# A PEER transformer layer on one core: low halves of early expert tiles made by a product, two PSUM banks for gates, one lookup traced later

## The chip, the core and the metric

The kernel runs on one core of a Trainium2 chip. The core has five engines with one instruction queue each: TensorE (PE, matrix products, with weight loads shown as PEld), VectorE (DVE), ScalarE (ACT), GpSimd (POOL) and SyncE (SP), and 16 DMA engines that all queues share. Each engine works off its queue in order; work on different engines is ordered by semaphores. The metric is the device time of one execution in microseconds (us), lower is better; of several runs the median counts.

## The reference

One layer of a diffusion backbone over 1024 latent tokens and 256 context tokens of width 1024. After the token mixers and their projection, `x1 = x + ...`, comes a PEER feed-forward part, the part that matters here:

```
h2 = modulate(rmsnorm(x1))                       # 1024 x 1024
q  = h2 @ wq                                     # 8 heads, two halves of 128
s1, s2 = q halves against 128 keys each;  top 16 of each half
cand = 16 x 16 sums per head;  top 16 of them    # 8 heads x 16 = 128 experts per token
gate = softmax(top 16);  expert = 128*i1 + i2    # of 16384 experts
act  = gelu(h2 . u[expert])                      # u, v: 16384 x 1024 each
out  = sum over the 128 chosen of gate * act * v[expert]
```

The result is `rmsnorm(x1 + mod * out)`.

## The kernel before

Operands of the large products are split into two fp16 halves, high and low (`hi = fp16(s*x)`, `lo = fp16(s*x - hi)`), and `mm3` (L97) makes three fp16 products of them. The tokens are eight blocks of 128. After the mixers and the merge, a first choice (`choosing(0)`, then `route`, the lookup of expert numbers for one block) runs beside the merge and output projection of the second half of the tokens.

Then the feed-forward part is done in two ways at once:

* For blocks 2, 3, 5, 6, 7 (`DB`) densely. `u` is 128 tiles of 128 experts. For each tile `u_load` fetches it, `u_turn` transposes it on TensorE into two PSUM tiles `put` (four 128x128 transposes each) and makes `uT`, high and low halves; `u_act` multiplies it with `h2` (24 products of 256 columns into `ph0`, 24 of 384 into `ph1`) and takes gelu. The dense gates come from one-hot matrices: for four tokens at a time VectorE makes `oh` (two instructions), TensorE multiplies eight 128x128 products into one PSUM tile `pgm`, ScalarE copies it to `gs`. A block has 32 such groups.
* For blocks 0, 1, 4 (`GB`) by gathering. Each of 768 steps is an indirect DMA that GpSimd issues (a "gather": 128 rows of u or v, one per token, into one of `AHEAD` = 6 buffers `row`), and one VectorE instruction that uses it: a dot product with `h2n` for rows of u (L979), an accumulation into `gacc` for rows of v (L984).

An early stage (about 1900 to 2820 us in the profile) runs the gates of blocks 2 and 3, the second choice (`choosing(1)`, eight heads of top-16 searches on VectorE) and the gates of blocks 5, 6, 7. Between these a planner in the code slips in early u tiles: each step of the stage yields a price in us (1.65 for a group of gates, 3.3 and 1.5 in the choice, 14 for a lookup), and for each `U_US` = 6.5 us one `early_tile()` is traced, followed by `G_E` gathers on average. 75 tiles are made so and stored in `act_d`. A late stage (2890 to 4100 us) runs over 32 groups of four v tiles, splits them, weighs the activations (reloaded as `acr`) with the gates, multiplies (`pe`), adds on VectorE into `acc`, makes the remaining u tiles, and spreads the gathers that are left evenly.

The order of instructions on each engine is set by a scheduler that takes what is ready first. Two marks bind it: a gather's issue on GpSimd is queued behind `pace` (the last low-half subtraction of `u_turn`, also on GpSimd), and its use on VectorE behind `vmark`, the last gate or accumulation instruction.

`uf` (L1026) is a float32 copy of the scaled `put` in SBUF, from which GpSimd subtracts `hi` (L1027). `first_half` is the generator of the first choice and the lookups of blocks 0, 1 and 2; `CS` says how many of its steps are taken per merge step, per output-projection tile and in the norm.

Of the kernel before, what the change touches and what calls it, by code (L numbers as in the profile page):

```python
# [1 line left out]

# [16 lines left out]
P = 128  # L19
# [19 lines left out]
SU = 64.0  # L39
# [5 lines left out]
TB = 4  # L45
# [22 lines left out]
def tile_layer(ctx: ExitStack, tc: tile.TileContext, x, c, ctxt, c_ctx, ada_w, ada_b, norm_mix_g,  # L68
# [3 lines left out]
    V, S, G, PE = nc.vector, nc.scalar, nc.gpsimd, nc.tensor  # L72
# [30 lines left out]
    const = pool(ctx, "const")  # L103
    dram = pool(ctx, "dram", space=DRAM)
    ident = const.tile([P, P], F32, name="ident")
    make_identity(nc, ident)
    ones = const.tile([P, P], F32, name="ones")
    V.memset(ones, 1.0)
    eps = const.tile([P, 1], F32, name="eps")
    V.memset(eps, EPS)  # L110
# [62 lines left out]
    with ExitStack() as mixers:  # L173
# [704 lines left out]
        def out_proj(hf, yT, fill=None):  # L878
            tiles = []
            for i in range(4):  # L880
                n = hf * 4 + i
                xt = mg.tile([P, D], F32, name=f"xr{n}", tag="xr", bufs=4)
                ld(out=xt, in_=x[n * P:(n + 1) * P, :])
                for h2 in range(2):
                    cs = slice(h2 * 512, (h2 + 1) * 512)
                    ps = pp.tile([P, 512], F32, name=f"pso{n}_{h2}", tag="pj", bufs=2)
                    mm3(ps, lambda k: yT[:, k, 0, i * P:(i + 1) * P], lambda k: yT[:, k, 1, i * P:(i + 1) * P],
                        lambda k: wo[:, 0, k, cs], lambda k: wo[:, 1, k, cs])
                    tm = mg.tile([P, 512], F32, name=f"tm{n}_{h2}", tag="tm")
                    tt(V, tm, ps, mod2[:, cs], ALU.mult)  # L890
                    tt(G, xt[:, cs], xt[:, cs], tm, ALU.add)
                st_(out=x1_d[n * P:(n + 1) * P, :], in_=xt)
                tiles.append(xt)
                if fill is not None:
                    for _ in range(CS[1]):
                        next(fill, None)
            return tiles

        def h2_rows(hf):
# [12 lines left out]

            return rows_of

        def next_norm(hf, tiles, fill=None):
            ss = rms_cols(tiles, mg, f"x1_{hf}")
            if fill is not None:
                for _ in range(CS[2]):
                    next(fill, None)
            norm_T(tiles, ss, lambda s, k: hb[hf][:, s, k, :], lambda k: cols2[:, 1, k:k + 1], lambda k: cols2[:, 0, k:k + 1],  # L920
                   mg, pp, f"m{hf}_", h2_rows(hf))

        yin = load_y(0)
        yT = mg.tile([P, KC, 2, HT], F16, name="yT0", tag="yT")
# [6 lines left out]
        yT = mg.tile([P, KC, 2, HT], F16, name="yT1", tag="yT")  # L931
# [8 lines left out]

        first_half = first()
        for j in range(KC):
            for _ in range(CS[0]):
                next(first_half, None)
            merge_step(1, j, yin, yT)
        next_norm(1, out_proj(1, yT, first_half), first_half)
        for _ in first_half:
            pass
        if "x1" in dbg:
# [22 lines left out]
    def gathering():  # L972

        held = []

        def use(n, s, row, h2n, dots):
            with tc.issue_after(vmark[0].ins):
                if h2n is not None:
                    V.scalar_tensor_tensor(out=row, in0=row, scalar=1.0, in1=h2n, op0=ALU.mult, op1=ALU.mult,  # L979
                                           accum_out=dots[:, s:s + 1])  # L980
                elif s == 0:
                    tsc(V, gacc[n], row, dots[:, s:s + 1], ALU.mult)
                else:
                    V.scalar_tensor_tensor(out=gacc[n], in0=row, scalar=dots[:, s:s + 1], in1=gacc[n],  # L984
                                           op0=ALU.mult, op1=ALU.add)
            if h2n is not None and s == P - 1:
                S.activation(dots, dots, AF.Gelu)
                tt(V, dots, dots, gsel[n][1], ALU.mult)

        for n in GB:  # L990
            h2n = pq.tile([P, D], F32, name=f"h2n{n}", tag="h2n")
            ld(out=h2n, in_=h2_d[GB.index(n)])
            dots = pq.tile([P, P], F32, name=f"dots{n}", tag="dots")
            for src, hh in ((peer_u, h2n), (peer_v, None)):
                for s in range(P):
                    if len(held) == AHEAD:
                        use(*held.pop(0))
                    row = pq.tile([P, D], F32, name=f"row{n}_{s}_{hh is None}", tag="row", bufs=AHEAD)
                    with tc.issue_after(pace[0].ins):
                        G.indirect_dma_start(out=row, out_offset=None, in_=src[0],  # L1000
                                             in_offset=bass.IndirectOffsetOnAxis(ap=gsel[n][0][:, s:s + 1], axis=0))
                    held.append((n, s, row, hh, dots))
                    yield
        for h in held:
            use(*h)
# [4 lines left out]
    def u_load(e):  # L1010
        un = pu.tile([P, D], F32, name=f"un{e}", tag="un", bufs=2)
        ld(out=un, in_=u_r[e])
        return un

    def u_turn(e, un):

        uT = pu.tile([P, 2, KC, P], F16, name=f"uT{e}", tag="uT", bufs=2)
        for q in range(2):
            pt = ppu.tile([P, 512], F32, name=f"put{e}_{q}", tag="put", bufs=2)
            for k in range(4):  # L1020
                PE.transpose(pt[:, k * P:(k + 1) * P], un[:, (q * 4 + k) * P:(q * 4 + k + 1) * P], ident)  # L1021
            pv = pt.rearrange("p (a b) -> p a b", a=4)
            hi, lo = uT[:, 0, q * 4:q * 4 + 4, :], uT[:, 1, q * 4:q * 4 + 4, :]
            S.activation(hi, pv, AF.Copy, scale=SU)  # L1024
            uf = pu.tile([P, 4, P], F32, name=f"uf{e}_{q}", tag="uf", bufs=2)
            S.activation(uf, pv, AF.Copy, scale=SU)  # L1026
            pace[0] = G.tensor_tensor(out=lo, in0=uf, in1=hi, op=ALU.subtract)  # L1027
        return uT

    def u_act(e, uT):  # L1030

        ac = pu.tile([P, TD], F32, name=f"ac{e}", tag="ac", bufs=3)
        o = 0
        for hf, (a, b) in enumerate(DH):
            cs, w = slice((a - hf * 4) * P, (b - hf * 4) * P), (b - a) * P
            ph = ppu.tile([P, w], F32, name=f"ph{hf}_{e}", tag=f"ph{hf}")
            mm3(ph, lambda k: uT[:, 0, k, :], lambda k: uT[:, 1, k, :],
                lambda k: h2h(hf, k)[:, cs], lambda k: h2l(hf, k)[:, cs])
            S.activation(ac[:, o:o + w], ph, AF.Gelu, scale=1.0 / (SU * SH2))  # L1039
            o += w  # L1040
        return ac


    with ExitStack() as st:
# [16 lines left out]
        def gate_block(rT, n, nb):  # L1061

            gs = pg.tile([P, P, NB], F32, name=f"gs{n}_{nb}", tag="gs", bufs=2)
            for t0 in range(0, NB, TB):
                c0 = nb * NB + t0
                oh = pg.tile([P, 4, P, TB], F16, name=f"oh{n}_{c0}", tag="oh", bufs=4)
                cols_ = lambda j: rT[:, j:j + 2, c0:c0 + TB].unsqueeze(2).to_broadcast([P, 2, P, TB])
                tt(V, oh[:, 0:2], iota.unsqueeze(1).to_broadcast([P, 2, P, TB]), cols_(0), ALU.is_equal)
                vmark[0] = V.tensor_tensor(out=oh[:, 2:4], in0=oh[:, 1:2].to_broadcast([P, 2, P, TB]), in1=cols_(2), op=ALU.mult)
                pgm = ppg.tile([P, TB, P], F32, name=f"pgm{n}_{c0}", tag="go")  # L1070
                for t in range(TB):
                    for j in (2, 3):
                        PE.matmul(pgm[:, t, :], lhsT=oh[:, 0, :, t], rhs=oh[:, j, :, t], start=j == 2, stop=j == 3)  # L1073
                S.activation(gs[:, :, t0:t0 + TB].rearrange("p i n -> p n i"), pgm, AF.Copy, scale=SA / SG)  # L1074
                yield 1.65
            st_(out=G_d[DB.index(n) * (P // NB) + nb], in_=gs)
# [29 lines left out]
        def early_tile():  # L1106
            nonlocal uT, pend
            e = pend
            pend = next(es, None)
            uTn = u_turn(pend, u_load(pend)) if pend is not None else None  # L1110
            ac = u_act(e, uT)
            st_(out=act_d[early.index(e)], in_=ac)
            uT = uTn

# [158 lines left out]
```

## Time and profile before

| | |
|---|---|
| median of 3 runs | 4191.13 us (4185.23 to 4202.76) |
| the profiled execution | 4186.54 us, its span 4184.8 us |
| mean granted TensorE clock | 0.971 |
| PE / DVE / ACT / POOL busy over the span | 93% / 71% / 34% / 39% |
| DMA | 884.66 MB, mean 211 GB/s |

The span runs from the first to the last instruction; what lies around it is 1.7 us. Busy shares are means over stages with different limits, so they are to be read by stage. PE's busy time counts the pipeline's tail of a product, so that a product before a wait looks longer than one in a stream.

### The profile page before, as it was taken

Reading aid. Unit: us, or ns where it says so; the run is one execution under the profiler, and the core shown is the slowest. Engines: PE = TensorE matmul, PEld = TensorE weight load, DVE = VectorE, ACT = ScalarE, POOL = GpSimd, SP = SyncE. Lnnn points to the kernel's source line nnn. Section 1 sums busy time; section 2 is a strip of 40 time slices with the busy share of each in tenths; the row PEclk is TensorE's granted clock in tenths of the full one; section 3 lists DMA queues with packets and bytes.
Section 4 is the critical chain, followed back from the end, with each engine's and each line's share of the span. In section 5 each row is a group of like instructions: output and inputs, shape, how many; then the busy total and the mean of one; then the engine's idle time right before and its main releaser. Section 6 shows DMA issues by size and latency. Waiting matters only on the chain.

```text
span 4184.8 us, 60506 instructions
## 1 busy us (share of the span) xinstructions
PE 3875.4 (93%) x23802; PEld 2352.4 (56%) x23802; DVE 2961.0 (71%) x5292; ACT 1417.9 (34%) x2186; POOL 1624.5 (39%) x1197
## 2 busy tenths in 40 slices
PE   6999999999999999978999988897999999999997
PEld 2665666656565444436766656675555554554553
DVE  5345446343546513688889899995889898889999
ACT  5335344242333202115532344553222222222222
POOL 2111111010111002016666577765555465555553
PEclk8999999999999999999999999999999999999999
DMA  5222122221323573317887778898999998988997
GB/s 191 73 79 86 46 81 82 63 85 46 91 71 108 162 261 125 116 57 270 328 309 276 248 254 314 307 335 310 310 316 321 314 318 308 323 289 304 319 309 247
DMA packets 435308, 884.66 MB, mean 211 GB/s; under 512 B 28512, under 2 KB 245067, under 8 KB 431439
## 3 DMA queue, kind: packets, MB, share of 16 engines
q0 software_dynamic: 110592, 402.70, 27.7%
q1 hardware_dynamic: 202676, 320.19, 22.8%
q10 hardware_dynamic: 121754, 157.89, 10.8%
q8 instruction: 187, 3.06, 0.3%
q14 instruction: 99, 0.80, 0.1%
HBM read 764.80 MB, written 115.88 MB: 210 GB/s over the span
## 4 chain that ended last, share of the span: by engine, by line
PE 39%; DVE 30%; DMA 10%; issue 10%; ACT 5%; POOL 4%; SPq 0%; ACTq 0%; DVEq 0%; POOLq 0%
DVE gacc L984 7%; DVE row_False L979 4%; PE ph L100 4%; DMA acr<-act_d 3%; DMA row_False<-in_peer_u_dram,idx 3%; PE pj_f0h L100 3%; PE pv_g L100 3%; PE pv_h L100 2%; PE pgm L1073 2%; PE pj_f1h L100 2%; PE pj_m L100 2%; DVE acc L1168 2%; POOL row_False L1000 2%; DVE v L94 2%; PE pq L100 2%
## 5 line engine op out<-in xcount | busy, mean ns | idle before, releaser
L100 PE MATMUL ph<-hb,uT 128*128 128x256 f16 (+1 forms) x6144 | 905.1, 304 | 44.6 <-POOL uT L1027 33.6
L100 PE MATMUL pe<-v,w 128*128 128x512 f16 x3840 | 864.2, 385 | 70.2 <-DVE acc L1168 65.4
L100 PEld LDWEIGHTS <-uT 128*128 128x128 f16 x6144 | 614.0, 100 | 271.1 <-POOL uT L1027 37.4
L100 PEld LDWEIGHTS <-w 128*128 128x128 f16 x3840 | 380.5, 99 | 541.1 <-issue 105.2
L1000 POOL DMA_INDIRECT row_True<-in_peer_v_dram,idx x384 | 482.3, 1256 | 360.2 <-DVE gacc L984 293.4
L1000 POOL DMA_INDIRECT row_False<-in_peer_u_dram,idx x384 | 504.8, 1315 | 267.8 <-DVE row_False L979 174.0
L979 DVE SCALAR_TENSOR_TENSOR row_False<-row_False,h2n 128x1024 f32<-128x1024 f32 x384 | 520.9, 1389 | 70.1 <-DMA row_False<-in_peer_u_dram,idx 60.2
L984 DVE SCALAR_TENSOR_TENSOR gacc<-row_True,dots,gacc 128x1024 f32<-128x1024 f32 x381 | 535.0, 1404 | 22.6 <-DMA row_True<-in_peer_v_dram,idx 21.1
L1027 POOL TENSOR_TENSOR uT<-uf,uT 128x512 f16<-128x512 f32 x256 | 379.3, 1494 | 200.3 <-ACT uf L1026 197.9
L93 ACT ACTIVATE v<-vn 128x1024 f16<-128x1024 f32 x128 | 135.1, 1056 | 495.4 <-DMA vn<-in_peer_v_dram 368.6
L1074 ACT ACTIVATE gs<-pgm 128x512 f32<-128x512 f32 x160 | 171.8, 1074 | 167.2 <-PE pgm L1073 160.1
L94 DVE SCALAR_TENSOR_TENSOR v<-vn,v 128x1024 f16<-128x1024 f32 x128 | 176.5, 1380 | 54.2 <-ACT v L93 54.2
L1073 PE MATMUL pgm<-oh 128*128 128x128 f16 x1280 | 176.7, 295 | 40.4 <-ACT gs L1074 26.3
L1039 ACT ACTIVATE ac<-ph 128x256 f32<-128x256 f32 (+1 forms) x256 | 109.6, 440 | 289.6 <-PE ph L100 258.3
L1168 DVE TENSOR_TENSOR acc<-pe,acc 128x512 f32<-128x512 f32 x310 | 206.6, 683 | 0.8 <-PE pe L100 0.8
L100 PE MATMUL pj_m<-hb,w_m 128*128 128x512 f16 x768 | 182.3, 393 | 2.3 <-DVE lf_g L86 1.6
L1073 PEld LDWEIGHTS <-oh 128*128 128x128 f16 x1280 | 144.9, 116 | 67.6 <-issue 45.5
L100 PE MATMUL pq<-hb,w_wq 128*128 128x512 f16 x768 | 177.1, 384 | 1.0 <-POOL hb L89 0.7
L1024 ACT ACTIVATE uT<-put 128x512 f16<-128x512 f32 x256 | 153.7, 600 | 69.0 <-PE put L1021 61.6
L1026 ACT ACTIVATE uf<-put 128x512 f32<-128x512 f32 x256 | 155.1, 606 | 25.5 <-POOL uT L1027 25.1
L100 PEld LDWEIGHTS <-hb 128*128 128x128 f16 x1536 | 150.3, 98 | 17.7 <-issue 0.3
L89 POOL TENSOR_TENSOR lf_g<-lf_g,ab_g 128x1280 f32<-128x1280 f32 x8 | 23.1, 2890 | 336.3 <-ACT ab_g L639 336.3
(364 smaller groups left out, 5649.8 us busy)
## 6 DMA issues: line engine op xcount, KB each, us to landing
un<-in_peer_u_dram SPq DMA_DIRECT2D x128, 512.0 KB
vn<-in_peer_v_dram SPq DMA_DIRECT2D x128, 512.0 KB
G_d<-gs ACTq DMA_DIRECT2D x20, 2048.0 KB
gt<-G_d ACTq DMA_DIRECT2D x32, 1280.0 KB
act_d<-ac ACTq DMA_DIRECT2D x80, 320.0 KB
acr<-act_d SPq DMA_DIRECT2D x80, 320.0 KB
mw<-in_ada_w_dram SPq DMA_DIRECT2D x32, 512.0 KB
w_wq<-wq_d SPq DMA_DIRECT2D x32, 512.0 KB
```

The lines of the kernel that those rows point to most:

```text
L93: S.activation(hi, src, AF.Copy, scale=float(scale))
L94: return V.scalar_tensor_tensor(out=lo, in0=src, scalar=float(scale), in1=hi, op0=ALU.mult, op1=ALU.subtract)
L100: PE.matmul(ps, lhsT=a(k), rhs=b(k), start=n == 0, stop=n == last)
L979: V.scalar_tensor_tensor(out=row, in0=row, scalar=1.0, in1=h2n, op0=ALU.mult, op1=ALU.mult, accum_out=dots[:, s:s + 1])
L984: V.scalar_tensor_tensor(out=gacc[n], in0=row, scalar=dots[:, s:s + 1], in1=gacc[n], op0=ALU.mult, op1=ALU.add)
L1000: G.indirect_dma_start(out=row, out_offset=None, in_=src[0], in_offset=bass.IndirectOffsetOnAxis(ap=gsel[n][0][:, s:s + 1], axis=0))
L1024: S.activation(hi, pv, AF.Copy, scale=SU)
L1026: S.activation(uf, pv, AF.Copy, scale=SU)
L1027: pace[0] = G.tensor_tensor(out=lo, in0=uf, in1=hi, op=ALU.subtract)
L1073: PE.matmul(pgm[:, t, :], lhsT=oh[:, 0, :, t], rhs=oh[:, j, :, t], start=j == 2, stop=j == 3)
L1074: S.activation(gs[:, :, t0:t0 + TB].rearrange("p i n -> p n i"), pgm, AF.Copy, scale=SA / SG)
L1168: vmark[0] = V.tensor_tensor(out=acc[n][:, hs], in0=ps, in1=acc[n][:, hs], op=ALU.add)
```

## The change

1. In the early stage the low half of a u tile is no longer made from `uf` by GpSimd. A constant `nid` (the identity times -1/SU, fp16) is made once; for each `put` tile TensorE adds `nid`ᵀ·`hi` (one 128x512 product) onto the transposed tile, and ScalarE reads the remainder, scaled by SU, as `lo`. For that the transposes become one accumulation group. These steps (`ends`) are traced inside `u_act` of the previous tile, between its two products. The first tile and the tiles of the late stage keep the old way.
2. `pace` is so set once by the first tile and then not again until the late stage.
3. `pgm` has two PSUM buffers instead of one.
4. `G_E` goes from 4.2 to 4.6.
5. `CS` becomes the single number 9; the lookup of block 2 is traced behind the norm instead of in the third output-projection tile. In the scheduled programs the rows of that lookup stand in the same place on every engine: up to the first gates nothing but the making of `nid` differs.
6. `ones` shrinks from 128x128 to 128x1.

```
-G_E = 4.2
-CS = (9, 1, 1)
+G_E = 4.6
+CS = 9
...
+    nid = const.tile([P, P], F16, name="nid")
+    tsc(V, nid, ident, -1.0 / SU, ALU.mult)
...
-                if fill is not None:
-                    for _ in range(CS[1]):
-                        next(fill, None)
+                if fill is not None and i < 2:
+                    next(fill, None)
...
-        next_norm(1, out_proj(1, yT, first_half), first_half)
+        next_norm(1, out_proj(1, yT, first_half))
...
-    def u_turn(e, un):
+    def u_turn(e, un, ends=None):
+        def low(pt, pv, hi, lo):
+            PE.matmul(pt, lhsT=nid, rhs=hi.rearrange("p a b -> p (a b)"), start=False, stop=True, skip_group_check=True)
+            S.activation(lo, pv, AF.Copy, scale=SU)
...
-                PE.transpose(pt[:, k * P:(k + 1) * P], un[:, (q * 4 + k) * P:(q * 4 + k + 1) * P], ident)
+                PE.matmul(pt[:, k * P:(k + 1) * P], lhsT=un[:, (q * 4 + k) * P:(q * 4 + k + 1) * P], rhs=ident,
+                          is_transpose=True, start=k == 0, stop=k == 3)
             S.activation(hi, pv, AF.Copy, scale=SU)
+            if ends is not None:
+                ends.append(lambda a=(pt, pv, hi, lo): low(*a))
+                continue
             uf = pu.tile([P, 4, P], F32, name=f"uf{e}_{q}", tag="uf", bufs=2)
             S.activation(uf, pv, AF.Copy, scale=SU)
             pace[0] = G.tensor_tensor(out=lo, in0=uf, in1=hi, op=ALU.subtract)
...
-    def u_act(e, uT):
+    def u_act(e, uT, ends=()):
...
+            if hf == 0:
+                for f in ends:
+                    f()
...
-                pgm = ppg.tile([P, TB, P], F32, name=f"pgm{n}_{c0}", tag="go")
+                pgm = ppg.tile([P, TB, P], F32, name=f"pgm{n}_{c0}", tag="go", bufs=2)
...
-            uTn = u_turn(pend, u_load(pend)) if pend is not None else None
-            ac = u_act(e, uT)
+            ends = []
+            uTn = u_turn(pend, u_load(pend), ends) if pend is not None else None
+            ac = u_act(e, uT, ends)
```

On TensorE, at a tile in the gates of block 2, the queue before (products `ph` of one tile, `put` transposes of a later one, `pgm` gates) reads:

```order
L100 MATMUL ph_8_15327<-hb_86,uT_15139 128x384
...
L1073 MATMUL pgm_64_15371<-oh_64_15368 128x128
...
L1021 MATMUL put_0_15423<-ident,un_15420 128x128 x4
L1021 MATMUL put_1_15432<-ident,un_15420 128x128 x4
...
L100 MATMUL ph_10_15442<-hb_85,uT_15281 128x256
...
L1073 MATMUL pgm_68_15384<-oh_68_15381 128x128
```

and now:

```order
L100 MATMUL ph_8_15290<-hb_87,uT_15139 128x256
...
L1019 LDWEIGHTS nid
L1019 MATMUL put_0_15277<-uT_15276,nid 128x512
L1019 LDWEIGHTS nid
L1019 MATMUL put_1_15283<-uT_15276,nid 128x512
...
L100 MATMUL ph_8_15320<-hb_88,uT_15139 128x384
...
L1084 MATMUL pgm_64_15367<-oh_64_15364 128x128
...
L1084 MATMUL pgm_68_15380<-oh_68_15377 128x128
...
L1025 MATMUL put_0_15419<-ident,un_15416 128x128 x4
L1025 MATMUL put_1_15425<-ident,un_15416 128x128 x4
```

Two products with `nid` stand between the two halves of a tile's `ph`, and two groups of gates now stand side by side. Over the early stage there are 148 such products from the first gate product to the last and 150 in all.

On GpSimd, in the gates of block 2 and 3, two subtractions stood between each four or five gathers:

```order
L1027 TENSOR_TENSOR uT_16823<-uf_0_16830,uT_16823 128x512
L1027 TENSOR_TENSOR uT_16823<-uf_1_16839,uT_16823 128x512
L1000 DMA row_67_False<-in_peer_u_dram,idx_14582 128x1024
L1000 DMA row_68_False<-in_peer_u_dram,idx_14582 128x1024
L1000 DMA row_69_False<-in_peer_u_dram,idx_14582 128x1024
L1000 DMA row_70_False<-in_peer_u_dram,idx_14582 128x1024
L1027 TENSOR_TENSOR uT_16962<-uf_0_16969,uT_16962 128x512
```

Now nothing stands between the gathers but the eight casts of the second choice (`idf`, one a head, each waiting for its head's search `ii` on VectorE); the sixth, seventh and eighth cast stand side by side:

```order
L998 DMA row_97_False<-in_peer_u_dram,idx_14584 128x1024
L788 CAST idf_17050<-ii_0_17123 128x8x16
L998 DMA row_98_False<-in_peer_u_dram,idx_14584 128x1024
...
L998 DMA row_73_True<-in_peer_v_dram,idx_14584 128x1024
L788 CAST idf_17050<-ii_5_19182 128x8x16
L788 CAST idf_17050<-ii_6_19594 128x8x16
L788 CAST idf_17050<-ii_7_20006 128x8x16
L998 DMA row_74_True<-in_peer_v_dram,idx_14584 128x1024
```

On VectorE, inside the second choice, runs of eight or nine uses of gathered rows alternated with a head's search:

```order
L979 SCALAR_TENSOR_TENSOR row_98_False,dots_14728<-row_98_False,h2n_14726 128x1024
L979 SCALAR_TENSOR_TENSOR row_99_False,dots_14728<-row_99_False,h2n_14726 128x1024
L758 MAX vv_2_17962<-s_2_17891 128x8 x2
...
L760 MATCH_REPLACE wk_2_31_18096<-vv_2_17962,s_2_17891 128x128
L979 SCALAR_TENSOR_TENSOR row_100_False,dots_14728<-row_100_False,h2n_14726 128x1024
```

Now the runs are of 12 to 17, one a head up to the fifth search, and after the sixth search (`vv_5`) has begun no use follows for 205 rows, until the lookups:

```order
L982 SCALAR_TENSOR_TENSOR gacc_14546<-row_66_True,dots_14728,gacc_14546 128x1024
L760 MAX vv_5_19181<-s_5_19110 128x8 x2
...
L982 SCALAR_TENSOR_TENSOR gacc_14546<-row_67_True,dots_14728,gacc_14546 128x1024
L761 MAX_INDEX ii_5_19182<-vv_5_19181,s_5_19110 128x8
...
L814 SCALAR_TENSOR_TENSOR t1r_20563<-abur_20559,t1r_20563 128x128
L982 SCALAR_TENSOR_TENSOR gacc_14546<-row_68_True,dots_14728,gacc_14546 128x1024
```

Uses per part of the early stage, counted on VectorE's queue: gates of blocks 2 and 3, 69 before and 76 now; from there to the first gate of block 5, 117 and 129; to the last gate, 118 and 129. Of the lookups' rows 56 stood in the second part and 54 in the third; now 94 and 16.

## Rows read from the trace of the kernel before

**Rows 1.** Busy time by stretch: length, engines, then PEclk, DMA share, GB/s.

```profile
1900.00:2115.00 215.00, 200.83 (x1526) 160.99 (x1525) 188.92 (x272) 118.04 (x178) 149.56 (x110) 1.00 0.85 317
2115.00:2474.00 359.00, 322.30 (x2113) 216.82 (x2112) 316.06 (x1035) 111.39 (x215) 231.09 (x184) 0.97 0.78 267
2474.00:2818.00 344.00, 308.57 (x2272) 243.16 (x2271) 335.38 (x415) 178.17 (x266) 252.95 (x175) 0.97 0.88 314
...
2890.00:4100.00 1210.00, 1145.18 (x6191) 616.22 (x6191) 1077.85 (x1283) 329.76 (x523) 681.85 (x522) 0.98 0.90 312
```

**Rows 2.** Waits of PE, 1900 to 2115: total us, times, longest us.

```profile
PE pgm L1073 <- ACT gs L1074: 11.5, 31, 0.6
```

**Rows 3.** Waits of PE, then of DVE, 2115 to 2474.

```profile
PE ph L100 <- POOL uT L1027: 24.1, 10, 4.8
...
DVE gacc L984 <- DMA row_True<-in_peer_v_dram,idx: 21.1, 14, 3.9
```

**Rows 4.** Waits of PE, 2474 to 2818.

```profile
PE pgm L1073 <- ACT gs L1074: 14.5, 39, 0.5
PE pgm L1073 <- DVE oh L1069: 9.5, 6, 3.2
PE ph L100 <- POOL uT L1027: 9.5, 4, 3.8
```

**Rows 5.** Waits of PE, then of DVE, 2890 to 4100.

```profile
PE pe L100 <- DVE acc L1168: 59.0, 33, 5.3
...
DVE acr L89 <- DMA acr<-act_d: 51.2, 27, 7.3
```

**Rows 6.** Single tiles, 1900 to 2830: min/median/max ns, first and last start.

```profile
L979 DVE SCALAR_TENSOR_TENSOR row_False<-row_False,h2n x181: 1199/1217/3903, 1914.6 to 2823.2; 128x1024 f32<-128x1024 f32 x181
...
L984 DVE SCALAR_TENSOR_TENSOR gacc<-row_True,dots,gacc x127: 1266/1275/3840, 2294.8 to 2676.5; 128x1024 f32<-128x1024 f32 x127
...
L1069 DVE TENSOR_TENSOR oh<-oh,rTr x160: 666/680/4242, 1900.1 to 2817.7; 128x1024 f16<-128x1024 f16 x160
```

**Rows 7.** Groups by line, DVE, 1900 to 2830: count, busy us, mean ns.

```profile
L979 DVE SCALAR_TENSOR_TENSOR row_False<-row_False,h2n 128x1024 f32<-128x1024 f32 x181 | 259.5, 1467 | 42.4 <-DMA row_False<-in_peer_u_dram,idx 32.5 <-issue 9.5
L984 DVE SCALAR_TENSOR_TENSOR gacc<-row_True,dots,gacc 128x1024 f32<-128x1024 f32 x127 | 188.4, 1484 | 21.5 <-DMA row_True<-in_peer_v_dram,idx 21.1
L1069 DVE TENSOR_TENSOR oh<-oh,rTr 128x1024 f16<-128x1024 f16 x160 | 123.5, 792 | 0.6
L89 DVE TENSOR_TENSOR oh<-iota,rTr 128x1024 f16<-128x1024 f16 x159 | 121.4, 787 | 12.9 <-PE pgm L1073 10.2 <-ACT gs L1074 2.0 <-issue 0.3
```

**Rows 8.** Timeline from 1902: DVE, then POOL (start us, us).

```profile
1907.02 3.23 DVE L1069 TENSOR_TENSOR oh<-oh,rTr 128x1024 f16<-128x1024 f16 x2
...
1902.20 7.50 POOL L1027 TENSOR_TENSOR uT<-uf,uT 128x512 f16<-128x512 f32 x4 [9.49 <-ACT uf L1026]
```

**Rows 9.** The page's groups: a 512-column product, and ScalarE's two copies.

```profile
L100 PE MATMUL pq<-hb,w_wq 128*128 128x512 f16 x768 | 177.1, 384 | 1.0 <-POOL hb L89 0.7
...
L1024 ACT ACTIVATE uT<-put 128x512 f16<-128x512 f32 x256 | 153.7, 600 | 69.0 <-PE put L1021 61.6
L1026 ACT ACTIVATE uf<-put 128x512 f32<-128x512 f32 x256 | 155.1, 606 | 25.5 <-POOL uT L1027 25.1
```

**Rows 10.** The page's DMA queues: packets, MB, share of 16 engines (the gathers).

```profile
q0 software_dynamic: 110592, 402.70, 27.7%
```

**Rows 11.** Timeline of DVE from 2420: half a lookup, its first and last row.

```profile
2420.14 1.21 DVE L89 TENSOR_TENSOR eqr<-iota,abfr 128x2048 f16<-128x2048 f16 x1
...
2425.68 2.92 DVE L89 TENSOR_TENSOR selr<-eqr 128x128 f32<-128x128 f16 x1
```

**Rows 12.** Timeline of DVE from 2294: a run of nine uses, first and last rows.

```profile
2294.77 1.27 DVE L984 SCALAR_TENSOR_TENSOR gacc<-row_True,dots,gacc 128x1024 f32<-128x1024 f32 x1
...
2310.71 3.38 DVE L984 SCALAR_TENSOR_TENSOR gacc<-row_True,dots,gacc 128x1024 f32<-128x1024 f32 x2 [0.33 <-DMA row_True<-in_peer_v_dram,idx]
```

**Rows 13.** Busy time of a short stretch, columns as in the first group.

```profile
2125.00:2150.00 25.00, 25.00 (x175) 17.24 (x173) 18.87 (x87) 7.73 (x16) 17.24 (x17) 1.00 1.00 384
```

More of the change, by code (lines that the diff above doesn't have):

```diff
@@ L1 @@
-from contextlib import ExitStack
+from contextlib import ExitStack, nullcontext
 import concourse.bass as bass
@@ L106, in tile_layer @@
     make_identity(nc, ident)
-    ones = const.tile([P, P], F32, name="ones")
+    nid = const.tile([P, P], F16, name="nid")
+    tsc(V, nid, ident, -1.0 / SU, ALU.mult)
+    ones = const.tile([P, 1], F32, name="ones")
     V.memset(ones, 1.0)
@@ L913, in h2_rows, with next_norm @@
             return rows_of
-        def next_norm(hf, tiles, fill=None):
+        def next_norm(hf, tiles):
             ss = rms_cols(tiles, mg, f"x1_{hf}")
-            if fill is not None:
-                for _ in range(CS[2]):
-                    next(fill, None)
             norm_T(tiles, ss, lambda s, k: hb[hf][:, s, k, :], lambda k: cols2[:, 1, k:k + 1], lambda k: cols2[:, 0, k:k + 1],
@@ L942, in tile_layer @@
         for j in range(KC):
-            for _ in range(CS[0]):
+            for _ in range(CS):
                 next(first_half, None)
             merge_step(1, j, yin, yT)
-        next_norm(1, out_proj(1, yT, first_half), first_half)
+        next_norm(1, out_proj(1, yT, first_half))
         for _ in first_half:
@@ L998, in gathering @@
                     row = pq.tile([P, D], F32, name=f"row{n}_{s}_{hh is None}", tag="row", bufs=AHEAD)
-                    with tc.issue_after(pace[0].ins):
+                    with tc.issue_after(pace[0].ins) if pace[0] is not None else nullcontext():
                         G.indirect_dma_start(out=row, out_offset=None, in_=src[0],
```

## The prediction

> **What bounds the kernel now.** I read busy time by stretch first, then the waits in each stretch, then single instructions. Up to 1900 us nothing is queued otherwise, so only what follows counts. I cut the early stage where VectorE's gate instructions stop and start again: gates of blocks 2 and 3 (A, 1900 to 2115), second choice (B, to 2474), gates of blocks 5 to 7 (C, to 2818), then a passage of 72 us and the late stage [rows 1].
>
> In A TensorE is busy 200.8 of 215 us; its main wait is for ScalarE to empty the one gate bank, 11.5 us in 31 pieces [rows 2]. In B VectorE is busy 316 of 359, TensorE 322 [rows 1]; TensorE waits 24.1 us for GpSimd's subtraction, VectorE for gathered rows [rows 3]. In C VectorE is busy 335 of 344, TensorE 309, the DMA engines 0.88: VectorE sets the end, and TensorE waits for the bank, for VectorE's one-hot tiles and for the subtraction, 33.5 us [rows 1, 4]. The late stage is TensorE's: 1145 of 1210 busy, and the rest, 59 us, is mostly waits for VectorE's accumulation, behind which stands VectorE's own wait for reloaded activations, 51 us [rows 1, 5].
>
> **The change part by part.**
>
> *Subtractions off GpSimd (150 of them).* What they cost is paid on VectorE. Its two-input instructions have tight medians, 1217, 1275 and 680 ns [rows 6], but means of 1467, 1484, 792 and 787 [rows 7]. Where four subtractions stand on GpSimd, two one-hot instructions beside them take 3.23 us [rows 8], against twice 0.68. With the second one-hot line at its twin's median the excess is 0.250·181 + 0.209·127 + 0.112·160 + 0.107·159 = 45 + 27 + 18 + 17 = 107 us. I let it go whole, split by length: A 25, B 42, C 40. TensorE's waits for the subtraction go as well.
>
> *The products.* 36 in A, 58 in B, 54 in C. A 512-column product is busy 177.1/768 = 0.23 us in a stream and 0.384 from start to end [rows 9]; the trace has none that waits for ScalarE just before, so the bounds are these two. I take 0.23, since 20 products of the other tile stand between the high half and this one: A 8, B 13, C 12 us. On ScalarE the second reading of the bank replaces the copy, 600 ns for 606 [rows 9]: nothing. The new wait, of the next tile's transposes for that reading, has 24 products of 384 columns before it; uncovered it would cost 0.6 us a bank, 90 us in all, which I don't expect.
>
> *Two gate banks.* The waits for ScalarE go: 11.5 us in A, 14.5 in C.
>
> *G_E 4.6.* 30 gathers move from the late stage to the early one: 7, 12 and 11 more uses in A, B, C. Each costs VectorE 1.22 to 1.28 us [rows 6] and the DMA engines 0.277·4184.8/768 = 1.51 us [rows 10].
>
> *The order that follows.* No longer behind subtractions, gathers are used earlier in B, in runs of about 16, one a head for five heads; then three heads go without. 38 rows of lookup also move from C into B. Half a lookup takes 8.5 us [rows 11], a lookup (27 rows) 17, so 38 rows are 24 us.
>
> *The lookup behind the norm and* ones: nothing, since the queues show the same order.
>
> **The sum.** A is TensorE's: 215 − 11.5 + 8 = 211.5. Busy time also counts the tail before each of 31 waits, so I take 209, **−6** (bounds −14, all idle gone, and +8).
>
> B is VectorE's: 316 − 42 + 12·1.25 + 24 = 313 us of work. What it waits depends on a gather's pace p within a run. Per head 21 gathers are used; six have landed during the search. The search itself is what is left of 316 − 42 after 117 uses (143) and 56 rows of lookup (35): 96/8 = 12 us. So a head takes 12 + 6·1.22 + 15p. For p there are two rows: the DMA engines' 1.51, and a run of nine uses in 2314.1 − 2294.8 = 19.3 us, 2.1 each [rows 12], which had subtractions in it. Five heads take 210 to 254, the 12 uses before them 16 to 20, the three heads without gathers, 3.5 lookups and 16 uses 36 + 60 + 20 = 116: 342 to 390 in all. With p = 1.8, the middle, 365: **+6** (bounds −17, +31). TensorE needs 322 − 24 + 13 = 311 and will wait at B's end for the first gates of block 5.
>
> C: VectorE falls to 335 − 40 + 13 − 24 = 284, so TensorE is left: 344 − 33.5 + 12 = 322.5. The DMA engines need 0.88·344 + 11·1.51 = 320 us, nearly the same; such a load is borne only for short, 1.00 at 384 GB/s over 25 us [rows 13]. I take 328, **−16** (bounds −37, at the work alone, and 0).
>
> C moves 314 GB/s · 344 us + 11·0.524 MB = 114 MB, at 384 GB/s 296 us. The Trainium skill, page "SBUF — State Buffer", section "Summary: rules for kernel authors", says to reckon with about 358 GB/s between HBM and SBUF. By that rule, as an estimate, C could not end before 318 us and would stay within my term; the row above is higher than the rule over 25 us, and no row here shows it held for 300.
>
> The passage of 72 us: nothing changes in it, 0. In the late stage VectorE loses 38 us of work in 1078 and the DMA engines 45 in 1089. TensorE gains only what its 59 us of waits lose; these hang on reloads that come a little sooner. I take a sixth, **−10** (bounds 0, and −45, all of the DMA time).
>
> Together −6 + 6 − 16 − 10 = −26. The profiled execution took 4186.5 us, its span 4184.8; this gives 4160.5. The median of three runs lay 4.6 us above it, so I write **4162 us**, 0.7% under the median. Less than 0.5%, 21 us, can't be told from no change here.
>
> **Rivals.**
>
> *More is freed* (4098). The runs go at p = 1.51, B at 342 (−17), C at 312 (−32) because two engines have slack, A −10, the late waits halve, −30: −89. For it: contention is 107 us of VectorE's time in stretches where it is busiest. Against it: C would need 365 GB/s for 312 us, which no long stretch shows, and which the skill's 358 forbids; so I give it less than the excess alone would earn. 0.17.
>
> *Nothing comes of it* (4188). The DMA engines and VectorE's runs take back what is freed: A 0, B +20, C −13, late −5, in all +2. For it: A's DMA share of 0.85 with 7 more gathers, B's runs. The lookup edit, which does nothing, belongs here. 0.20.
>
> *The runs stall VectorE* (4235). In-order queues make B one chain: a use waits for its gather, that for a buffer six uses back, and GpSimd's cast of one head holds the gathers behind it. If a run goes at the late stage's pace (464 uses in 1210 us, 2.6), a head takes 58 us, B 5·58 + 23 + 116 = 429, +70; with A −6, C −16 and late 0: +48. It turns slower from p = 2.0 on without a gain in the late stage, from 2.1 with it. For it: VectorE's 21 us of waits on v rows now [rows 3]. Against it: with the subtractions gone GpSimd has only to issue. 0.11.
>
> **How the numbers follow.** My forecast has 0.52, its own range 4140 to 4178; about six in ten of that lies beyond 0.5%. Faster: 0.32 + 0.17 + 0.03 of the second rival = 0.52. Slower: 0.11 + 0.04 = 0.15. The rest, 0.33, is the same. The range for 8 in 10 cuts off half of the first and most of the third rival: 4108 to 4200.
>
> **What would show it.** The uses at their medians in A to C, and means within 30 ns of these, show the first step right. TensorE's waits for ScalarE's bank and GpSimd's subtraction must be gone in A and C; a wait of transposes for the second reading would be the uncovered cost. In B VectorE's waits for rows, in five clusters, and a wait of TensorE of some 40 us at the first gates of block 5 show the order's price; if B ends before 345 or after 385 us of length, my p was wrong. If C takes more than 340 with the DMA share over 0.95, the gathers were moved to where there was no room. The late stage's wait for the accumulation should stand near 49 us.

## The result: 1.1% faster

The changed kernel takes 4140.8 us (median of four runs, 4133.6 to 4152.1) against 4188.2 us (four runs), a ratio of 0.9888 with a 95% interval of 0.9861 to 0.9915. The profiled execution is the slowest of the four: 4152.1 us, span 4150.3, so the two traces differ by 34.5 us where the medians differ by 47. The busy time by stretch, columns as in [rows 1]; the stretches are gates of blocks 2 and 3 (A), second choice (B), gates of blocks 5 to 7 (C), the passage and the late stage:

```profile
1902.00:2109.00 207.00, 201.67 (x1524) 161.71 (x1523) 169.60 (x286) 114.11 (x172) 110.83 (x83) 0.98 0.90 345
2109.00:2480.00 371.00, 330.16 (x2203) 222.61 (x2201) 307.44 (x1079) 115.91 (x225) 170.18 (x139) 0.95 0.76 281
2480.00:2794.00 314.00, 305.38 (x2322) 245.29 (x2323) 276.93 (x418) 172.48 (x262) 174.80 (x129) 0.99 0.93 358
2794.00:2867.00 73.00, 61.45 (x425) 44.42 (x424) 36.34 (x39) 32.05 (x56) 37.38 (x25) 0.92 0.87 307
2867.00:4065.00 1198.00, 1135.87 (x6166) 612.37 (x6165) 1044.69 (x1224) 325.01 (x515) 625.88 (x492) 0.98 0.88 302
```

C is TensorE's now (305 of 314 us busy, VectorE 277), where it was VectorE's (335 of 344). From the first to the last one-hot instruction of a stretch (the second of each pair), A is 9 us shorter, B 11 longer, C 29 shorter; from first to last output product the late stage is 8 shorter, the passage 3; the start is 3 us later.

VectorE's two-input instructions from 1902 to 2800 us, columns as in [rows 7]:

```profile
L977 DVE SCALAR_TENSOR_TENSOR row_False<-row_False,h2n 128x1024 f32<-128x1024 f32 x210 | 249.7, 1221 | 81.6 <-DMA row_False<-in_peer_u_dram,idx 75.8 <-issue 5.0
L982 DVE SCALAR_TENSOR_TENSOR gacc<-row_True,dots,gacc 128x1024 f32<-128x1024 f32 x127 | 162.7, 1281 | 26.3 <-DMA row_True<-in_peer_v_dram,idx 21.2 <-issue 3.6 <-DVE gacc L982 0.3
L1080 DVE TENSOR_TENSOR oh<-oh,rTr 128x1024 f16<-128x1024 f16 x160 | 105.8, 687 | 0.6
L89 DVE TENSOR_TENSOR oh<-iota,rTr 128x1024 f16<-128x1024 f16 x160 | 105.5, 687 | 11.4 <-PE pgm L1084 9.6 <-ACT rTr L1068 1.1 <-issue 0.2
```

The means stand at the medians of [rows 6]: the excess over them is gone whole. TensorE's waits in A and in C, then VectorE's and TensorE's in the late stage (total us, times, longest us), against [rows 2, 4, 5]:

```profile
PE pgm L1084 <- ACT gs L1085: 2.5, 1, 2.5
PE ph L100 <- POOL uT L1035: 2.5, 1, 2.5
...
PE pgm L1084 <- DVE oh L1080: 8.8, 2, 5.9
...
DVE acr L89 <- DMA acr<-act_d: 55.8, 26, 9.0
PE pe L100 <- DVE acc L1180: 55.7, 34, 4.4
```

The waits for the bank and for the subtraction are gone but for one each; the late stage's wait for the accumulation is nearly what it was, 55.7 us for 59.0. In B TensorE has one wait that the kernel before didn't have, and VectorE waits for rows and for scores:

```profile
ACT dots L985 <- DVE row_False L977: 40.0, 1, 40.0
...
PE psc L755 <- ACT qT L752: 35.5, 1, 35.5
...
DVE row_False L977 <- DMA row_False<-in_peer_u_dram,idx: 23.8, 18, 5.6
...
DVE vv L760 <- ACT s L756: 17.2, 2, 12.9
...
DVE gacc L982 <- DMA row_True<-in_peer_v_dram,idx: 15.8, 17, 2.3
```

The timelines of ScalarE, TensorE and SyncE's queue show how it comes about (start us, us):

```profile
2183.38 0.33 ACTq L1124 DMA_DIRECT2D act_d<-ac  x1
2223.30 0.31 ACT L985 ACTIVATE dots<-dots 128x128 f32<-128x128 f32 x1 [39.95 <-DVE row_False L977]
2223.52 0.58 ACT L752 ACTIVATE qT<-pq 128x512 f32<-128x512 f32 x1
...
2182.66 5.34 PE L100 MATMUL pq<-hb,w_wq 128*128 128x512 f16 x24
2187.84 0.82 PE L1025 MATMUL put<-ident,un 128*128 128x128 f32 x6
2224.15 2.08 PE L755 MATMUL psc<-kT,qT 128*128 128x128 f32 x8 [35.49 <-ACT qT L752]
2226.02 7.46 PE L100 MATMUL pq<-hb,w_wq 128*128 128x512 f16 x24
...
2175.90 0.33 SPq L1010 DMA_DIRECT2D un<-in_peer_u_dram  x1
2223.30 0.33 SPq L990 DMA_DIRECT2D h2n<-h_d  x1
```

The gelu of block 0's 128 dot products (`dots`) needs the 128th use of a gathered row. It stands in ScalarE's queue ahead of the third head's `qT` (ScalarE's copy of that head's queries, from which TensorE makes the scores `psc`, which VectorE searches, `vv`); the use comes at 2222 us, and until then ScalarE does nothing, and TensorE nothing after 2188. SyncE's queue stands behind the same use with the load of the next block's `h2n`. Before, `dots` waited 6.2 us. TensorE's first products after the wait are slow, too: 24 `pq` in 7.46 us, against 5.34.

### The profile page after: what moved, and what is told of

Its sections match the earlier page's. It is cut to its first block, busy times and chain, and to the rows that moved or that the text cites. A ratio compares the mean times of both kernels' runs of the same rounds, so it can differ in the third digit from the quotient of the medians.

```text
span 4150.3 us, 60646 instructions
## 1 busy us (share of the span) xinstructions
PE 3881.3 (94%) x23952; PEld 2361.9 (57%) x23952; DVE 2840.1 (68%) x5293; ACT 1412.0 (34%) x2186; POOL 1390.0 (33%) x1047
## 4 chain that ended last, share of the span: by engine, by line
PE 45%; DVE 26%; issue 10%; DMA 10%; ACT 5%; POOL 4%; SPq 0%; ACTq 0%; DVEq 0%; POOLq 0%
PE ph L100 6%; DVE gacc L982 6%; DVE row_False L977 4%; DMA acr<-act_d 3%; PE pq L100 3%; PE pj_f0h L100 3%; DMA row_False<-in_peer_u_dram,idx 3%; PE pv_g L100 3%; POOL row_False L998 2%; PE pv_h L100 2%; DMA vn<-in_peer_v_dram 2%; PE pj_f1h L100 2%; PE pj_m L100 2%; DVE v L94 2%; DVE acc L1180 2%
## 5 line engine op out<-in xcount | busy, mean ns | idle before, releaser
L100 PE MATMUL ph<-hb,uT 128*128 128x256 f16 (+1 forms) x6144 | 891.3, 301 | 7.8 <-ACT ac L1047 5.0
L998 POOL DMA_INDIRECT row_True<-in_peer_v_dram,idx x384 | 462.3, 1204 | 438.7 <-DVE gacc L982 325.8
L977 DVE SCALAR_TENSOR_TENSOR row_False<-row_False,h2n 128x1024 f32<-128x1024 f32 x384 | 469.3, 1252 | 133.2 <-DMA row_False<-in_peer_u_dram,idx 127.4
L982 DVE SCALAR_TENSOR_TENSOR gacc<-row_True,dots,gacc 128x1024 f32<-128x1024 f32 x381 | 506.6, 1330 | 27.1 <-DMA row_True<-in_peer_v_dram,idx 21.2
L94 DVE SCALAR_TENSOR_TENSOR v<-vn,v 128x1024 f16<-128x1024 f32 x128 | 189.4, 1484 | 45.2 <-ACT v L93 44.4
L1035 POOL TENSOR_TENSOR uT<-uf,uT 128x512 f16<-128x512 f32 x106 | 166.8, 1587 | 131.9 <-ACT uf L1034 131.0
L1025 PE MATMUL put<-ident,un 128*128 128x128 f32 x1024 | 136.7, 276 | 8.3 <-ACT uf L1034 6.2
```

What stands on the lines that cost most here:

```text
L94: return V.scalar_tensor_tensor(out=lo, in0=src, scalar=float(scale), in1=hi, op0=ALU.mult, op1=ALU.subtract)
L100: PE.matmul(ps, lhsT=a(k), rhs=b(k), start=n == 0, stop=n == last)
L998: G.indirect_dma_start(out=row, out_offset=None, in_=src[0], in_offset=bass.IndirectOffsetOnAxis(ap=gsel[n][0][:, s:s + 1], axis=0))
L1025: PE.matmul(pt[:, k * P:(k + 1) * P], lhsT=un[:, (q * 4 + k) * P:(q * 4 + k + 1) * P], rhs=ident, is_transpose=True, start=k == 0, stop=k ...
```

## The experiments

Theory 1: GpSimd's subtractions held VectorE, and their going is the gain. Theory 2: it is the second gate bank. Theory 3: the 30 earlier gathers. Theory 4, formed on the trace above: B's loss is the queues that stand behind the 128th use. Each ratio is to the kernel before as measured beside that run (medians from 4185.3 to 4189.9 us). Lengths are in us, of the profiled executions, from mark to mark as above.

| | median us | ratio to before, 95% | A | B | C | late |
|---|---|---|---|---|---|---|
| before | 4188 | | 215 | 361 | 341 | 1266 |
| after | 4141 | 0.9888 (0.9861–0.9915) | 206 | 372 | 313 | 1258 |
| e1 products only | 4178 | 0.9981 (0.9972–0.9990) | 218 | 361 | 322 | 1273 |
| e2 banks only | 4217 | 1.0075 (1.0062–1.0088) | 221 | 366 | 346 | 1276 |
| e3 gathers only | 4209 | 1.0057 (1.0041–1.0073) | 225 | 378 | 362 | 1253 |
| e4 products, banks | 4149 | 0.9912 (0.9899–0.9925) | 195 | 368 | 301 | 1273 |
| e5 subtractions back | 4234 | 1.0120 (1.0105–1.0136) | 218 | 413 | 348 | 1253 |
| e6 products twice | 4159 | 0.9936 (0.9923–0.9950) | 208 | 382 | 319 | 1257 |
| e7 gelu later | 4139 | 0.9885 (0.9870–0.9900) | 199 | 371 | 311 | 1257 |
| e8 uses spread | 4113 | 0.9828 (0.9814–0.9841) | 202 | 344 | 309 | 1253 |
| e9 subtractions free | 4201 | 1.0035 (1.0023–1.0047) | 222 | 381 | 344 | 1256 |
| e10 gelu and load later | 4121 | 0.9834 (0.9822–0.9847) | 201 | 352 | 312 | 1253 |
| e11 more gathers in B | 4096 | 0.9779 (0.9766–0.9791) | 202 | 351 | 307 | 1238 |
| e12 products late too | 4125 | 0.9846 (0.9833–0.9859) | 203 | 350 | 307 | 1260 |

**The parts by themselves.**

e1 is the changed kernel with `G_E = 4.2` and one `pgm` buffer.

> The products with the scaled identity (and the lookup and `ones` edits, which move no instruction) without the second gate bank and without the 30 more early gathers (G_E 4.2, one pgm buffer). Theory 1 (GpSimd's subtractions held VectorE, and their going is the gain): means of VectorE's two-input instructions in the early stage fall to their medians (1220, 1280, 684 ns); TensorE's waits for the one bank stay, 11.5 us in A and some 14.5 in C, so 4141 + 20 = about 4160 us (4150 to 4170). Theory 2 (the second bank is the gain): within 8 us of 4188.

4178: a miss for theory 1's size, though the means are near the medians here too (1228, 1279, 695 and 687 ns). C fell from 341 to 322, A grew by 3. TensorE and VectorE wait for each other through the one bank; in C:

```profile
DVE oh L89 <- PE pgm L1084: 37.2, 39, 3.8
PE pgm L1084 <- ACT gs L1085: 16.4, 45, 0.5
```

e2 is the kernel before with `tag="go", bufs=2`.

> The kernel before with two pgm buffers and nothing else. Theory 1: TensorE's bank waits go, but C stays VectorE's (busy 335 of 344 us) and B too, so only A may shorten by up to 11 us: 4178 to 4190 us. Theory 2: C shortens by some 20 us and A by 9, about 4155 us.

4217, slower by 31 us: theory 2 falls, and my bound of 4190 with it. The wait for the bank became one for VectorE, in A and in C:

```profile
PE pgm L1073 <- DVE oh L1069: 21.0, 11, 4.3
...
PE pgm L1073 <- DVE oh L1069: 29.0, 23, 5.4
```

The slower time is clear (six runs, 4212 to 4223 us), its cause is not. In the profile the loss is some 5 us in each of A, B, C and the passage and 10 in the late stage, whose code is the same. What of it is the order and what the spread of profiles (the late stage has 1266 to 1276 in the four kernels with `G_E = 4.2`) stays open.

e3 is the kernel before with `G_E = 4.6`.

> The kernel before with G_E 4.6 and nothing else: 30 gathers earlier. Theory 1: B and C are VectorE's before the products, and 24 more uses there cost 1.45 us each (means with the subtractions in them), 35 us, against 8 to 10 us won in the late stage: 4205 to 4220 us. Theory 3 (the early gathers are the gain, since the late stage is short of DMA): 4150 to 4175 us. The price of 30 gathers in the late stage is read from its length against 1265.7 us.

4209, in theory 1's range: theory 3 falls. Early, 30 gathers cost 46 us where VectorE sets the end (A +9, B +16, C +21), and give back 13 late.

e4 is the changed kernel with `G_E = 4.2`.

> The changed kernel with G_E back at 4.2. Theory 1: the early stage is TensorE's now, so taking 30 gathers out of it gives little there (C a few us, B up to 12 by its shorter runs), and the late stage gets back its 8 us: 4135 to 4150 us. Theory 3: 4170 us or more.

4149, as theory 1 had it: two parts that give −7 and +31 us alone give −36 together. In A and C TensorE hardly stands still:

```profile
1900.00:2095.00 195.00, 194.47 (x1493) 156.78 (x1491) 163.45 (x271) 110.81 (x169) 102.20 (x76) 1.00 0.92 345
...
2462.00:2764.00 302.00, 300.35 (x2294) 241.65 (x2295) 264.53 (x374) 168.88 (x257) 168.35 (x117) 0.99 0.93 351
```

Against it the 30 gathers of the full change lengthen the early stage by 27 us and shorten the late one by 16 in the profiles; the medians differ by 8 with overlapping intervals. (Its profiled run, 4137, lies as far under its median as that of the changed kernel lies over its own.)

**Is it the port, or the wait?** e5 puts subtractions back that nobody needs:

```
 ends.append(lambda a=(pt, pv, hi, lo): low(*a))
+du = pu.tile([P, 4, P], F32, ..., tag="uf", bufs=2)
+G.tensor_tensor(out=du, in0=<128x128 constant, 4 times>, in1=hi, op=ALU.subtract)
```

> The changed kernel, with a GpSimd subtraction of the old size (128x512, fp32 less fp16) put back for each of the 150 halves; it reads the high half of the tile and writes a buffer that nobody reads, and no gather is queued behind it by a mark. Theory 1 (the subtractions cost by holding VectorE's two-input instructions): means of these rise again by 0.1 to 0.25 us, 100 us of VectorE's time over the early stage, C goes back to VectorE's and the whole to 4165 to 4190 us. Rival (what cost was TensorE's wait for the result and the gathers queued behind it): 4135 to 4150 us, as the changed kernel.

4234, beyond both. It mixes two costs: the subtractions read `hi` and so held the two `uT` buffers. In B ScalarE waited for them before it could write the next tile, and TensorE's products waited for ScalarE:

```profile
ACT uT L1029 <- POOL du L1033: 58.8, 9, 12.8
...
PE put L1019 <- ACT uT L1029: 37.2, 5, 10.5
```

e9 takes this away: `in1` is `nid`, and an order mark keeps the subtractions between the gathers.

> As e5, but the subtractions read only constants, so no buffer of a tile is held by them: they are queued on GpSimd behind the gathers by an order mark, nobody waits for them, and their results are used by nobody. Theory 1 (holding VectorE is what they cost): contention of 100 to 115 us on VectorE again, A 6 to 12 us longer than the changed kernel's, C 25 to 35 longer, B 0 to 20: 4175 to 4200 us. Rival (what e5 showed came from tile buffers that the subtractions held): 4141 to 4155 us.

4201, at the upper end of theory 1's range, 60 us over the changed kernel and over the kernel before too. Nobody uses what these subtractions make; VectorE's lines from 1898 to 2850 us:

```profile
L977 DVE SCALAR_TENSOR_TENSOR row_False<-row_False,h2n 128x1024 f32<-128x1024 f32 x208 | 266.3, 1324 | 44.4 <-DMA row_False<-in_peer_u_dram,idx 44.2
L982 DVE SCALAR_TENSOR_TENSOR gacc<-row_True,dots,gacc 128x1024 f32<-128x1024 f32 x127 | 190.5, 1500 | 21.7 <-DMA row_True<-in_peer_v_dram,idx 20.1 <-issue 0.2
L89 DVE TENSOR_TENSOR oh<-iota,rTr 128x1024 f16<-128x1024 f16 x160 | 144.3, 930 | 7.5 <-PE pgm L1088 7.2 <-issue 0.3
L1084 DVE TENSOR_TENSOR oh<-oh,rTr 128x1024 f16<-128x1024 f16 x160 | 135.4, 870 | 0.7
```

Against the means after, 208·0.103 + 127·0.219 + 160·0.243 + 160·0.183 = 21 + 28 + 39 + 29 = 117 us of VectorE are back, and A, B and C are 16, 9 and 31 us longer. The gathers behind the subtractions on GpSimd are not the cause: VectorE waits 44.2 + 20.1 us for rows here, less than the 75.8 + 21.2 of the changed kernel. The Trainium skill, page "SBUF — State Buffer", section "Who interferes with whom", says that a VectorE instruction with two inputs in SBUF and a GpSimd instruction that reads SBUF exclude each other, the later one standing still; these means agree.

**What bounds it now.** e6 doubles each product, with a matrix of zeros:

```
+PE.matmul(pt, lhsT=zid, rhs=..., start=False, stop=False, ...)
 PE.matmul(pt, lhsT=nid, rhs=..., start=False, stop=True, ...)
```

> The changed kernel with each product with the scaled identity preceded by one of the same size with a matrix of zeros into the same tile: 148 products of 512 columns more, 0.23 us each, some 8, 13 and 12 us in A, B, C. If TensorE sets the end in all three stretches: +34 us, 4175. If it does in A and C alone, and B's 35 us wait of TensorE swallows its share: +20, 4161. If VectorE or the DMA engines set the ends: under +8.

4159, +18.5, some half of what the added products take. In the profiles B is 10 longer than in the changed kernel, C 7, A 2 (some 7 against e7, e8 and e10, which have its gathers). TensorE is busy 205 of 208 us in A and 316 of 319 in C, so it sets the end there. In B its long wait is 34.0 us, hardly less than 35.5, so it did not take up B's share: after 2224 us TensorE sets the pace, which the profile's chain of the work that ended last shows for the changed kernel too (from 2222 to 2420 us it lies on TensorE, 78% on `ph` and `pq`).

**B's wait.** e7 moves one instruction:

```
+with tc.issue_after(smarks[1, 3].ins) if n == 0 else nullcontext():  # after head 3's scores
     S.activation(dots, dots, AF.Gelu)
```

> The changed kernel with one instruction moved: the gelu of block 0's 128 dot products (`dots`, on ScalarE) is queued behind the copies of the fourth head's scores. In the changed kernel it stands in ScalarE's queue ahead of the third head's qT, waits 40 us for the 128th use of a gathered row, and TensorE stands 35.5 us behind it in B. Theory 4 (that wait is B's loss, since TensorE sets the end of the whole early stage): B some 30 us shorter, 4105 to 4118 us. Rival (B is VectorE's chain of gathers, as the prediction had it): within 8 us of 4141.

4139, a miss: B stays at 371. The wait moved to the other queue (TensorE in B, then SyncE's queue):

```profile
PE put L1028 <- DMA un<-in_peer_u_dram: 23.0, 1, 23.0
...
SPq L993 <- DVE vv L762: 45.9, 1, 45.9
```

L993 loads `h2n`, which can't come before the last use of its predecessor; u tiles stand behind it. e10 moves that load, too:

```
+lmark[0] = ld(out=un, in_=u_r[e])
...
+with tc.issue_after(lmark[0].ins) ...:
     ld(out=h2n, in_=h2_d[GB.index(n)])
```

> As e7, and the load of block 1's h2n on SyncE queued behind the last u tile's load that is traced before it. In e7 that load stood in SyncE's queue ahead of u tiles and waited 46 us for the same 128th use, and TensorE stood 23 us for a u tile. Theory 4 (TensorE sets the end of the early stage, and any queue that stands behind the 128th use costs its whole wait): B 30 us shorter than 371, 4105 to 4115 us. Rival (B is VectorE's chain of gathers, and TensorE's wait only moves): B above 362, 4130 us or more.

4121: B loses 20 us and the time 19, less than the 30 expected. TensorE still has a third wait of the kind: a lookup's activation (`selr`) that stands on ScalarE ahead of a tile's `uT` and waits 18.5 us for VectorE, and TensorE behind it. But TensorE no longer sets B's end. VectorE's waits for scores (17.2 us above) are gone, its waits for rows are not, and the chain of the work that ended last (shares of B) names no line of TensorE among its largest: it goes from gather to row to use to search, as the prediction had B. First two waits on ScalarE and TensorE, then two of VectorE's, then the chain:

```profile
ACT selr L836 <- DVE selr L89: 26.3, 3, 18.5
...
PE put L1029 <- ACT uT L1024: 18.6, 2, 16.6
...
DVE row_False L979 <- DMA row_False<-in_peer_u_dram,idx: 21.3, 14, 3.9
DVE gacc L984 <- DMA row_True<-in_peer_v_dram,idx: 12.8, 13, 1.8
...
by line: issue 15.1%; DMA row_True<-in_peer_v_dram,idx 14.7%; DMA row_False<-in_peer_u_dram,idx 9.7%; DVE eqr L89 8.7%; DVE gacc L984 8.4%; DVE ii L763 4.7%; DVE ii L766 4.7%; DVE wk L764 4.7%; DVE row_False L979 4.4%; POOL row_False L1002
```

e8 goes at the order itself: the last search instruction of each `top16` sets `vmark`, so uses stand where they are traced.

```
-V.max_index(out=ids[:, 8:16], in_max=vals[:, 8:16], in_values=wk)
+vmark[0] = V.max_index(out=ids[:, 8:16], in_max=vals[:, 8:16], in_values=wk)
```

> The changed kernel with the mark for the uses of gathered rows also set by each search of the second choice, so that uses stand in the queue where they are traced, eleven to fourteen a head over all eight heads and the lookups, instead of 15 to 25 over five. Theory 4: the 128th use is then late by order, but ScalarE's gelu stands behind the scores of that head, and TensorE's 35 us wait goes: 4105 to 4120 us. Prediction's reading (the bunched runs at the gathers' pace are what lengthens B): also shorter, by the row waits in B, 24 + 16 = 40 us of VectorE's, at most 12 us of B's length: about 4130 us.

4113, in theory 4's range. TensorE is busy 335 of 343 us in B (second row; A and C around it). Two things went at once, though: TensorE's wait and VectorE's waits for rows, 39.6 us in the changed kernel and 0.6 here, so that e8 alone does not tell which it was. Only now does B's chain lie on TensorE (last row):

```profile
1900.00:2102.00 202.00, 199.21 (x1528) 160.80 (x1527) 168.10 (x286) 115.28 (x173) 110.41 (x83) 0.99 0.94 356
2102.00:2445.00 343.00, 335.43 (x2253) 226.89 (x2252) 289.01 (x1042) 114.67 (x225) 179.09 (x137) 1.00 0.82 297
2445.00:2755.00 310.00, 299.71 (x2276) 240.68 (x2274) 292.20 (x454) 175.68 (x261) 185.53 (x130) 0.98 0.97 369
...
DVE row_False L978 <- DMA row_False<-in_peer_u_dram,idx: 0.6, 1, 0.6
...
by line: PE ph L100 40.7%; PE pq L100 22.5%; DVE gacc L983 6.3%; DVE eqr L89 5.4%; PE psc L755 5.3%; PE put L1026 5.2%; issue 5.0%; PE put L1020 2.8%; ACT qT L752 1.2%; DVE wk L762 0.5%; DVE selr L89 0.5%; DVE ii L764 0.4%; DVE vv L763 0.4%
```

**A better version, and where the edit stops paying.** e11 is e8 with gathers per early tile by stage:

```
-G_E = 4.6
+G_E = (4.4, 5.6, 4.4)
```

> As e8, with 4.4 gathers per early tile in the gates and 5.6 in the second choice, some 20 more uses early in all, since e8 shows the DMA engines busy 0.82 in B and 0.97 in C. If free DMA time in B takes them and C is held by the DMA engines: A and C 2 to 5 us shorter each, B as before, the late stage 8 to 10 us shorter: 4095 to 4105 us. If B's searches or GpSimd can't take them: B longer by 10 to 20 us, 4113 to 4125 us.

4096, 2.2% under the kernel before and the fastest here. B took 25 more uses for 7 us, C's length fell by 3, and the late stage's by 15. B and C:

```profile
2102.00:2452.00 350.00, 342.73 (x2309) 232.35 (x2307) 319.06 (x1069) 117.06 (x230) 204.47 (x162) 1.00 0.91 331
2452.00:2759.00 307.00, 290.35 (x2207) 233.90 (x2206) 288.34 (x471) 173.06 (x255) 177.69 (x128) 0.98 0.97 364
```

e12 is e11 with the products in the late stage as well (`u_turn(en, u_load(en), ends)` in `next_act`).

> As e11, and the low halves of the 53 u tiles of the late stage are made by the product with the scaled identity too, so GpSimd subtracts no more: 104 more products of 512 columns, 0.22 us each, 23 us of TensorE. In the late stage TensorE sets the end (busy 1154 of 1200 us in e11) and VectorE's 63 to 76 us of contention lie beside it. Theory 1 with its condition (contention costs only where VectorE sets the end): 23 us more, less at most half of TensorE's 51 us of gaps there: 4096 to 4118 us. Rival (contention costs wherever it stands, as TensorE's waits there are for VectorE's accumulation): those gaps go nearly whole, 4065 to 4085 us.

4125, 29 us slower than e11 and worse than theory 1's range. TensorE's waits in the late stage:

```profile
PE put L1020 <- ACT uT L1030: 35.7, 13, 10.0
...
PE pe L100 <- DVE acc L1185: 19.8, 15, 3.5
```

The wait for the accumulation halved (43.2 us in e11 over the same stage), but the products wait for ScalarE's high half, 35.7 us there and 19.2 more in the passage (of the changed kernel's 150 products one waited for ScalarE, 1.4 us). So 104 products, 23 us by the price above, come with new waits of 55 us, longer than the 23 that went.

## Why the prediction was right, and where not

4162 us was forecast, 4140.8 came, inside the range, 21 us or a half per cent under the forecast, and just inside the 4140 to 4178 that the likeliest case had as its own. (The sum, 4160.5, with the 4.6 us named beside it is 4165, not 4162.) In the pair of traces the change is −34.5 us for a sum of −26; most of the rest is that the changed kernel's profiled run lies 11 us over its median.

* *Subtractions off GpSimd, 107 us of VectorE let go whole.* Right: the means are at the medians, and e9 brings 117 us back. That C then falls to TensorE was right too, and e4 shows why it took two parts: without the bank TensorE is held by ScalarE (e1), without the products by VectorE (e2). I had priced the bank's waits as a term of their own; they are a condition.
* *Products.* 148 at about 0.22 us: two of them at 2354.06 us are followed 0.43 us later by the next product, and no transpose waits for the second reading in A or C.

```profile
2354.06 0.59 PE L1019 MATMUL put<-uT,nid 128*128 128x512 f16 x2
2354.49 4.06 PE L100 MATMUL ph<-hb,uT 128*128 128x384 f16 x24
```

* *A, −6.* −9. I took 2.5 us off for the tails of the products before 31 waits; at 0.384 − 0.23 = 0.15 us each [rows 9] they are, as an estimate, 5.
* *C, −16; this term was mis-sized, −29.* Two steps failed. The first left TensorE 322.5 us: C took 314, and TensorE was busy 305 of them, 3 less than before with 54 products more. I took no tails off here, though 49 waits went [rows 4], some 7 us by the same estimate; and the granted clock was 0.99 for 0.97. How much each gave isn't separated. The second added 5.5 us because the DMA engines were taken to need 320 us and to bear such a load only for short. They were busy 0.93·314 = 292 us, at 358 GB/s; in C of e8 it was 0.97·310 = 301 us, at 369. So neither [rows 13], which shows 25 us and no limit, nor the rule of 358 that I had set beside it was a wall. Another page of the Trainium skill, "Perfetto Trace Analysis", section "Roofline", says so: 358 is a core's share while its neighbour works as well, and a core alone can pull more, up to some 435; e8's row agrees. That the load is free isn't shown: e4, with 12 uses fewer in C, has 301 us for 313.
* *B, +6; +11, with half of the mechanism forecast.* VectorE's chain of gathers was there, and at the forecast pace: on VectorE's timeline a head with its 19 to 22 uses takes 44 to 50 us, and 12 + 6·1.22 + 15·1.8 is 46. With TensorE's wait out of the way (e10) this chain sets B's end, at 352 us for 365. What failed is the step that gave TensorE slack up to B's end, and a wait of some 40 us there. It waited 35.5 us at the third head's scores, behind a gelu that waits for one use, and the last heads' scores then came too late for VectorE, which waited 17.2 us for them from 2397 us on; at B's end TensorE did not wait. I read VectorE's and GpSimd's queues of the new order, and not what stands on ScalarE's and SyncE's behind the 128th use. So of the 28 us by which e8 shortens B, 20 are the queues' (e10); the other 8 came when the uses were spread, and whether the gathers' pace or the `selr` wait held them isn't separated. That the length stayed within 345 to 385 is partly luck: the chain was shorter than forecast, and a wait that I hadn't seen made up for it.
* *Late, −10.* −8 in this pair; the mean of before and e1, e2, e4 (1272) less that of after and e5 to e10 (1255) is 17. A price for 30 gathers of 8 to 17 us. The wait for the accumulation, which was to fall to 49 us, stood at 55.7.
* *Rivals.* "More is freed" had the right C (312) and the wrong B (342); e8 is nearest to it, at 4113 against its 4098. What I held against it, that no stretch shows 365 GB/s for 312 us, C itself all but showed. "Nothing comes of it" had B at +20 and C at −13: neither came. "The runs stall VectorE" wanted 58 us a head; queues that work in order did cost B, but on ScalarE and SyncE.

## What to carry to other kernels

An instruction that waits for the last of many steps (a reduction's end, a reload of a single buffer) belongs behind everything that doesn't need it, on every queue: after a change of order, look for such instructions on the engines the change didn't touch. Behind such a wait a second chain can lie nearly level, as VectorE's did here: moving the two instructions gave 20 us of B, and spreading the uses gave the rest. A contention that lengthens an engine's instructions is worth most where that engine sets the end, and together with the wait that is next in line: here one edit alone gave 7 us, the other alone cost 31, and both gave 36, so price two such edits as a pair. The same edit can cost time in a stage that TensorE bounds, as in e12.

## What the runs showed that I had not expected

Sixteen DMA engines at a share of 0.97, 369 GB/s, for 310 us, beside gathers, in a stretch no longer than the changed kernel's (e8). And what a long wait costs TensorE after its end: from 2226 to 2230 us, behind 35.5 us without work, the granted clock is 0.50 of full speed, the 1.2 GHz level, and 24 products take 7.46 us for 5.34.

```profile
2226.00:2230.00 4.00, 4.00 (x12) 1.50 (x10) 1.54 (x2) 0.59 (x1) 2.85 (x3) 0.50 0.94 350
```
